# A streaming-encoder block: operands of the banded attention split for two heads at once and copied by DMA, values of the recurrence split in one piece

## The chip, the cores and the metric

The kernel runs on one core of one Trainium2 chip. The metric is the device time of one execution in microseconds. The core has a matmul engine (TensorE, "PE" in the profile, its weight load "PEld"), a vector engine (VectorE, "DVE"), a scalar engine (ScalarE, "ACT"), GpSimd ("POOL") and SyncE ("SP"), which only starts transfers. Each engine works through its own instructions in order; semaphores hold an instruction until what it needs is done. Sixteen DMA engines do the transfers. SBUF is the on-chip memory of 128 partitions, PSUM the accumulator memory that matmuls write.

## What is computed

One layer of a hybrid block, for 512 frames of width 1024. From the reference, cut to the two branches that the change touches:

```python
h = rmsnorm(x, norm_mix_g[l])
proj = h @ w_in[l]
...
y_a = chunked_relpos_attention(a_q, a_k, a_v, rel_bias[l])
y_b = hgrn2_recurrence(b_q, b_f, b_i, b_g, lb_all[l], hgrn_norm_g[l])
y_c = mla_attention(c_q, c_kv, c_kr, positions, ...)
up = jnp.einsum('bsnw,nwd->bsnd', branches, w_branch[l])
gates = jax.nn.sigmoid(gate_logits.reshape(bsz, seq, N_BRANCH, D_MODEL))
x = x + jnp.sum(gates * up, axis=2) @ w_out[l]
h2 = rmsnorm(x, norm_ffn_g[l])
x = x + jnp.square(jax.nn.relu(h2 @ w_ff1[l])) @ w_ff2[l]
```

The banded branch (A) has eight heads of width 64. Its scores, per chunk of 64 queries, carry a bias by relative position:

```python
s = jnp.einsum('bqhd,bkhd->bhqk', q_blk, k_band).astype(jnp.float32) * scale + bias
...
p = jax.nn.softmax(s, axis=-1).astype(v.dtype)
return jnp.einsum('bhqk,bkhd->bqhd', p, v_band)
```

The recurrence (B) has eight heads too and works on chunks:

```python
state = (jnp.exp(last[:, :, 0, :])[..., None] * state
         + jnp.einsum('bhjd,bhjv->bhdv', k_b * jnp.exp(last - cum), v_b))
```

## The kernel before

**Precision.** Every matmul runs on pairs: an operand is split into a rounded high half (ScalarE copies it to the matmul type) and a low half (VectorE subtracts the high half from the source). `split` (L209) does both; three matmuls, high by high, high by low and low by high, give a product.

**Order.** TensorE's order is written out by hand. The projections, gates and branch outputs are cut into units of one or two matmuls, and `fill(n)` puts the next n of them between the steps of a branch, so that TensorE has dense work while a branch waits for other engines. The other engines' orders are made by a scheduler from the program's order, its priorities and its model of times; a tile pool with `bufs=n` gives out n buffers in turn, and an instruction that writes a buffer waits for the last readers of its former content. Weights come through GpSimd's queue: `load` and `convert` bring a block twice, the second time added onto the negated high half, which leaves the low half.

**The stretches.** The latent branch (C) runs first, to about 166 us of the span; then the banded branch (A), to about 272 us; then the recurrence (B), to about 500 us; then the output projection and the feed-forward part. During C and A, `fill` works on projections, during B on gates and branch outputs.

**A branch's heads** go through `attention` (L566). A step is one head and one of four blocks of 128 queries, t = 0 to 3, with 128(t+1) keys. A step does the scores (`scores_step`, L516): matmuls into the PSUM tile `sc`, then VectorE adds the bias table and takes the row minimum (`sb`, L529), ScalarE takes the exponential and the row sum (`p`, L532); VectorE normalises later (L536, L537). Two steps behind, `transpose_step` (L540) transposes `p` through PSUM tiles `tp` and splits them into `pTh` (ScalarE) and `pTl` (VectorE). When all four blocks of a head are transposed, `value_step` (L554) multiplies by the values into a PSUM tile `av`, which ScalarE and VectorE add up into `ya` (L563, L564; `yc` in the latent branch). `tp` and `av` share two PSUM buffers.

**The operands of a banded head** are made by `prep_a` (L789). A projection gives queries and keys of a pair of heads in one tile of 128 partitions each (`aqk`), a head in each half. A head's query tile (`QT`, four of them, shared with the latent branch) holds the high half of the scaled queries in one half of the partitions and the low half in the other; its key tiles (`KT`, two for each parity of the head) hold the high half twice, and the low half twice. So one matmul of 128 partitions does two of the products. `prep_a(h + 2)` is called when the last block of head h has its scores issued, and is used a head later. It also brings the head's bias table (128 KB) by SyncE into one of two buffers, and VectorE negates it in place (L804), fills its left half (L805) and masks a corner (L806). The buffer is free when L529 of head h, t = 3, has read the old table.

**The values** of A and B come from `project_nat` (L445) as four tiles `nat`, one for each block of 128 frames, of 512 channels. A's are split into `v2` before the banded heads. B's are split in `ew_keys` (L1021), once for each pair of heads, block by block, into `vh` and `vl`.

Of the kernel before, what the change touches and what calls it, by code (L numbers as in the profile page):

```python
# [9 lines left out]
F32 = mybir.dt.float32  # L10
F32R = mybir.dt.float32r
I32 = mybir.dt.int32
AF = mybir.ActivationFunctionType
ALU = mybir.AluOpType
# [3 lines left out]
S = 512  # L18
P = 128
NK = D // P  # L20
NST = S // P
# [4 lines left out]
SC_A = 0.125  # L26
# [112 lines left out]
def _body(ctx, tc, ap, dbgo):  # L139
    nc = tc.nc  # L140
    V, A, G, T = nc.vector, nc.scalar, nc.gpsimd, nc.tensor
# [6 lines left out]
    def f(t):  # L148
        return t.bitcast(F32)
# [12 lines left out]
    def acc(n="acc"):  # L162
        return ps.tile([P, S], F32, tag="acc", name=n, bufs=3)
# [45 lines left out]
    def split(hi, lo, src):  # L209
        A.copy(hi, src)  # L210
        V.tensor_tensor(lo, src, f(hi), ALU.subtract)
# [121 lines left out]
    with ExitStack() as st_ctx:  # L333
# [10 lines left out]
        for k in range(NK):  # L344
            t = st.tile([P, S], F32, tag="xt", name="xt", bufs=8)
# [75 lines left out]
        for i in range(4):  # L421
            t = fqt(f"c{i}")
# [22 lines left out]
        def project_nat(src, name, pool, out, halves=(0, 1)):  # L445

            def half_run(half):
                def run():
                    pz = [acc("pv").rearrange("p (a c) -> p a c", a=2) for _ in range(2)]
                    for k in range(NK):  # L450
                        if k % 4 == 0:
                            wh, wl = get()
                        c = slice(k % 4 * 256, k % 4 * 256 + 256)
                        for s in range(NST):
                            q = slice(s * P, (s + 1) * P)
                            mm3(pz[s // 2][:, s % 2], xg[k][0][:, q], xg[k][1][:, q], wh[:, c], wl[:, c],
                                k == 0 and s % 2 == 0, k == NK - 1, skip_group_check=True)
                            if s < 3 or k < NK - 1:
                                yield from (1, 1)[s % 2:]
                    for s in range(NST):  # L460
                        if half == 0:
                            out.append(pool[0].tile([P, S], F32, tag="nat", name=name, bufs=4))
                        A.activation(out[s][:, half * 256:half * 256 + 256], pz[s // 2][:, s % 2], AF.Copy,
                                     scale=rstdn[:, s:s + 1])
                    yield 1
                return run
            for half in halves:
                last = add([src[half, kk] for kk in range(2)], half_run(half))
            return last
# [123 lines left out]
    with ExitStack() as at_ctx:  # L593
# [137 lines left out]
        with ExitStack() as a_ctx:  # L731
            app = a_ctx.enter_context(tc.tile_pool(name="apool", bufs=2, reuse_waits="tile"))
            v2 = []
            for s in range(NST):
                t = ab.tile([P, 8, P], F32R, tag="v2", name="v2a", bufs=4)
                split(t[:, :, 0:64], t[:, :, 64:128], avn[s].rearrange("p (h d) -> p h d", d=64))
                v2.append(t)
            nat_stack.close()
            lsp = ls_stack.enter_context(tc.tile_pool(name="lsp", bufs=1, side="right", reuse_waits="tile"))
# [46 lines left out]

            aops = {}

            def prep_a(h):  # L789
                pr, par = h // 2, h % 2  # L790
                q, k = aqk[2 * pr], aqk[2 * pr + 1]
                a = slice(par * 64, par * 64 + 64)
                o = slice(64 - par * 64, 128 - par * 64)
                q1 = QT[h % 4]
                k1, k2 = KT[2 * par], KT[2 * par + 1]
                A.activation(q1[a], q[a], AF.Copy, scale=-SC_A)
                V.scalar_tensor_tensor(q1[o], q[a], -SC_A, f(q1[a]), ALU.mult, ALU.subtract)
                A.copy(k1[a], k[a])
                A.copy(k1[o], k[a])
                V.tensor_tensor(k2[a], k[a], f(k1[a]), ALU.subtract)  # L800
                V.tensor_copy(k2[o], f(k2[a]))
                bias = app.tile([P, S], F32, tag="bias", name="bias", bufs=2)
                nc.sync.dma_start(bias[:, 256:], ap['rel'][h])
                V.tensor_scalar(bias[:, 256:], bias[:, 256:], -1.0, None, ALU.mult)  # L804
                V.tensor_scalar(bias[:, :256], relc[:, h:h + 1].to_broadcast([P, 256]), -1.0, None, ALU.mult)  # L805
                V.memset(bias[0:64, S - 64:S], -NEG)  # L806
                aops[h] = [(q1, k1), (q1, k2)], (bias, app)
# [11 lines left out]
    with ExitStack() as h_ctx:  # L819
# [103 lines left out]
        def items(pr):  # L923
# [97 lines left out]
            def ew_keys():  # L1021
                vh = st['vh'] = hp.tile([P, 4, P], F32R, name="vh", bufs=1)
                vl = st['vl'] = hp.tile([P, 4, P], F32R, name="vl", bufs=1)
                for c in range(4):
                    split(vh[:, c], vl[:, c], bvn[c][:, vs])
                d = st['dk'] = hw("dk", 384)
                G.tensor_tensor(d.rearrange("p (c i) -> p c i", i=P), cv[:, 0:3, P - 1:P].to_broadcast([P, 3, P]),
                                cv[:, 0:3], ALU.subtract)
                A.activation(d, d, AF.Exp)
                V.tensor_tensor(d, d, kk[:, :384], ALU.mult)  # L1030
                el = st['el'] = hp.tile([P, 4], F32, tag="el", name="el")
                A.activation(el, cv[:, :, P - 1], AF.Exp)
# [247 lines left out]
```

## Time and profile before

| what | value |
|---|---|
| median of three runs | 961.58 us (961.29 to 964.99) |
| the profiled execution | 962.54 us |
| its span, from first to last instruction | 960.8 us |
| mean granted TensorE clock | 0.991 |
| HBM traffic | 114.05 MB read, 2.16 MB written |

The forecast is worked out against the profiled execution, which took 1.74 us more than its span and 0.96 us more than the median. The page cuts the span into 40 slices of 24 us. A digit is the busy share of a slice in tenths (9 is 90% or more), `PEclk` the granted clock, DMA the mean busy share of the 16 DMA engines.

```profile
PE   8889999988998999999999999999999999999995
PEld 6578898977877788888778888888888888888995
DVE  6488888777878969788562554544322234446745
ACT  7557778777766667667552443443322234342311
POOL 4422101111144434342122013000000000000032
PEclk9999999999999999999999999999999999999998
DMA  6865445655666474758689623223223232322402
```

Slices 0 to 6 are the start and the latent branch, 7 to 11 the banded branch, 12 to 20 the recurrence, the rest the feed-forward part. TensorE is at 90% or more in most slices; VectorE is at 70 to 90% up to slice 18. The parts of the page that carry the prediction, and the answers of the trace behind them, stand there.

### The profile page before, as it was taken

How to read it: one execution, taken by the hardware profiler on the slowest of the kernel's cores; microseconds unless marked ns; L12 is line 12 of the kernel's file. 1: busy time of each engine (PE TensorE's matmuls, PEld its weight loads, DVE VectorE, ACT ScalarE, POOL GpSimd, SP SyncE). 2: the span in 40 equal slices, each digit the busy share in tenths (PEclk: the TensorE clock that was granted, in tenths of full speed). 3: DMA queues.
4: the chain of work that ended last, by engine and by line, in shares of the span. 5: the costliest groups of instructions: out<-in, count | busy, mean ns of one | idle time of the engine just before them, and what ended most of it. 6: DMA issues, size and time to landing. Idle time of an engine off the chain costs nothing.

```text
span 960.8 us, 12589 instructions
## 1 busy us (share of the span) xinstructions
PE 919.2 (96%) x4682; PEld 774.6 (81%) x4682; DVE 595.2 (62%) x1134; ACT 494.5 (51%) x911; POOL 183.2 (19%) x248
## 2 busy tenths in 40 slices
PE   8889999988998999999999999999999999999995
PEld 6578898977877788888778888888888888888995
DVE  6488888777878969788562554544322234446745
ACT  7557778777766667667552443443322234342311
POOL 4422101111144434342122013000000000000032
PEclk9999999999999999999999999999999999999998
DMA  6865445655666474758689623223223232322402
GB/s 198 212 136 124 89 82 114 138 116 121 139 131 134 102 165 104 161 125 193 136 209 203 158 87 101 97 88 110 88 97 100 88 110 88 100 97 88 154 1 88
DMA packets 37181, 117.04 MB, mean 122 GB/s; under 512 B 4416, under 2 KB 8656, under 8 KB 37120
## 3 DMA queue, kind: packets, MB, share of 16 engines
q0 software_dynamic: 18496, 67.17, 33.3%
q1 hardware_dynamic: 18624, 49.06, 15.8%
q8 instruction: 37, 0.61, 0.3%
q14 instruction: 24, 0.20, 0.1%
HBM read 114.05 MB, written 2.16 MB: 121 GB/s over the span
## 4 chain that ended last, share of the span: by engine, by line
PE 69%; DVE 14%; issue 7%; DMA 4%; ACT 3%; POOL 2%; SPq 0%; DVEq 0%; POOLq 0%; ACTq 0%
PE p L226 12%; PE p L224 12%; PE p L225 12%; PE pg L323 3%; PE pg L319 3%; PE pg L321 3%; PE pj L323 2%; PE pj L319 2%; PE pj L321 2%; DMA bias<-in_rel 2%; PE sc L520 2%; PE po L225 2%; PE po L226 2%; PE po L224 2%; PE tp L545 1%
## 5 line engine op out<-in xcount | busy, mean ns | idle before, releaser
L220 DVE TENSOR_TENSOR wl<-wr,wh 128x1024 fp32r<-128x1024 f32 x66 | 80.8, 1224 | 144.7 <-ACT wh L219 140.6
L219 ACT CAST wh<-wr 128x1024 fp32r<-128x1024 f32 x66 | 69.5, 1053 | 173.9 <-PE p L225 136.4
L224 PE MATMUL p<-x2h,wh 128*128 128x512 f32 x256 | 100.0, 391 | 0.0
L226 PE MATMUL p<-x2h,wl 128*128 128x512 f32 x256 | 99.6, 389 | 0.0
L225 PE MATMUL p<-x2l,wh 128*128 128x512 f32 x256 | 99.6, 389 | 0.0
L277 ACT ACTIVATE wl<-wh 128x1024 fp32r<-128x1024 f32 x64 | 67.8, 1059 | 49.7 <-PE pg L323 28.1
L224 PE MATMUL p<-rh,wh 128*128 128x512 f32 (+1 forms) x224 | 83.7, 374 | 0.0
L225 PE MATMUL p<-rl,wh 128*128 128x512 f32 (+1 forms) x224 | 83.7, 374 | 0.0
L226 PE MATMUL p<-rh,wl 128*128 128x512 f32 (+1 forms) x224 | 83.7, 374 | 0.0
L323 PE MATMUL pg<-xgh,wl 128*128 128x512 f32 x192 | 76.9, 401 | 0.6 <-DMA wl<-in_w_g 0.6
L1261 POOL TENSOR_TENSOR xres<-xres,cst 128x256 f32<-128x256 f32 x16 | 13.1, 822 | 335.7 <-ACT fss L1256 309.6
L319 PE MATMUL pg<-xgh,wh 128*128 128x512 f32 x192 | 76.7, 400 | 0.0
L321 PE MATMUL pg<-xgl,wh 128*128 128x512 f32 x192 | 76.4, 398 | 0.0
L319 PE MATMUL pj<-xgh,wh 128*128 128x512 f32 x160 | 64.6, 404 | 2.6 <-ACT c L427 2.6
L321 PE MATMUL pj<-xgl,wh 128*128 128x512 f32 x160 | 65.4, 408 | 0.0
L323 PE MATMUL pj<-xgh,wl 128*128 128x512 f32 x160 | 64.0, 400 | 1.3 <-DMA wl<-in_w_aqk 1.3
L225 PEld LDWEIGHTS p<-x2l,wh 128*128 128x128 f32 x256 | 48.1, 188 | 10.2 <-issue 0.2
L224 PEld LDWEIGHTS p<-x2h,wh 128*128 128x128 f32 x256 | 48.1, 188 | 10.1 <-issue 0.2
L226 PEld LDWEIGHTS p<-x2h,wl 128*128 128x128 f32 x256 | 48.1, 188 | 10.0
L225 PEld LDWEIGHTS p<-rl,wh 128*128 128x128 f32 x224 | 42.2, 188 | 7.5
L226 PEld LDWEIGHTS p<-rh,wl 128*128 128x128 f32 x224 | 42.2, 188 | 7.5
L224 PEld LDWEIGHTS p<-rh,wh 128*128 128x128 f32 x224 | 42.2, 188 | 7.4
(380 smaller groups left out, 2398.0 us busy)
## 6 DMA issues: line engine op xcount, KB each, us to landing
wr<-in_w_ff SPq DMA_DIRECT2D x64, 512.0 KB, 3.3
wh<-in_w_g POOLq DMA_DIRECT2D x24, 512.0 KB, 4.0
wl<-in_w_g POOLq DMA_DIRECT2D x24, 512.0 KB, 5.9
wh<-in_w_br POOLq DMA_DIRECT2D x12, 512.0 KB, 3.7
wl<-in_w_br POOLq DMA_DIRECT2D x12, 512.0 KB, 5.7
wh<-in_w_aqk POOLq DMA_DIRECT2D x8, 512.0 KB, 4.5
wl<-in_w_aqk POOLq DMA_DIRECT2D x8, 512.0 KB, 6.6
wr<-in_w_out SPq DMA_DIRECT2D x8, 512.0 KB, 3.3
```

The lines of the kernel that those rows point to most:

```text
L219: A.copy(hi[:, :n], r[:, :n])
L220: (eng or G).tensor_tensor(lo[:, :n], r[:, :n], f(hi[:, :n]), ALU.subtract)
L224: T.matmul(out, wh, xh, start=start, stop=False, **kw)
L225: T.matmul(out, wh, xl, start=False, stop=False, **kw)
L226: T.matmul(out, wl, xh, start=False, stop=stop, **kw)
L277: A.activation(lo, f(hi), AF.Copy, scale=-1.0)
L319: T.matmul(out, wh, xh, start=start, stop=False, **kw)
L321: T.matmul(out, wh, xl, start=False, stop=False, **kw)
L323: T.matmul(out, wl, xh, start=False, stop=stop, **kw)
L520: T.matmul(sc[:, :n], l[:, t * P:(t + 1) * P], r[:, :n], start=i == 0, stop=i == len(scores) - 1)
L545: T.transpose(tp[:, o * P:(o + 1) * P], p[:, kt * P:(kt + 1) * P], ident)
L1261: G.tensor_tensor(x2[m][:, n], x2[m][:, n], g_fin[:, m:m + 1].to_broadcast([P, 256]), ALU.mult)
```

## The change

**Banded branch.** A new `split_a` splits queries and keys of a pair of heads in tiles of 128 partitions: the scaled high half and the low half of the queries (`aqh`, `aql`), high and low half of the keys (`akh`, `akl`). The tiles come from a pool of eight buffers, two pairs' worth. `prep_a` no longer computes operands. Six SyncE transfers of 64x512 elements (128 KB) for each head copy them from the pair's tiles to where the head's matmuls read them: one for each half of the query tile, two for each key tile. The bias table is brought as before, behind these in the program.

**Values.** `project_nat` writes one tile with four blocks of frames instead of four tiles; the reader of A's values follows. `ew_keys` splits the values of a pair of heads in one go of 128x512 instead of four of 128x128.

```diff
             def half_run(half):
                 def run():
+                    if half == 0:
+                        out.append(pool[0].tile([P, NST, S], F32, tag="nat", name=name, bufs=1))
...
                     for s in range(NST):
-                        if half == 0:
-                            out.append(pool[0].tile([P, S], F32, tag="nat", name=name, bufs=4))
-                        A.activation(out[s][:, half * 256:half * 256 + 256], pz[s // 2][:, s % 2], AF.Copy,
+                        A.activation(out[0][:, s, half * 256:half * 256 + 256], pz[s // 2][:, s % 2], AF.Copy,
                                      scale=rstdn[:, s:s + 1])
...
-                split(t[:, :, 0:64], t[:, :, 64:128], avn[s].rearrange("p (h d) -> p h d", d=64))
+                split(t[:, :, 0:64], t[:, :, 64:128], avn[0][:, s].rearrange("p (h d) -> p h d", d=64))
...
+            def split_a(pr):
+
+                q, k = aqk[2 * pr], aqk[2 * pr + 1]
+                qh, ql, kh, kl = late['a'] = [app.tile([P, S], F32R, tag="as", name=n, bufs=8)
+                                              for n in ("aqh", "aql", "akh", "akl")]
+                A.activation(qh, q, AF.Copy, scale=-SC_A)
+                V.scalar_tensor_tensor(ql, q, -SC_A, f(qh), ALU.mult, ALU.subtract)
+                split(kh, kl, k)
+
             def prep_a(h):
+
                 pr, par = h // 2, h % 2
-                q, k = aqk[2 * pr], aqk[2 * pr + 1]
+                if par == 0:
+                    split_a(pr)
+                qh, ql, kh, kl = late['a']
                 a = slice(par * 64, par * 64 + 64)
                 o = slice(64 - par * 64, 128 - par * 64)
                 q1 = QT[h % 4]
                 k1, k2 = KT[2 * par], KT[2 * par + 1]
-                A.activation(q1[a], q[a], AF.Copy, scale=-SC_A)
-                V.scalar_tensor_tensor(q1[o], q[a], -SC_A, f(q1[a]), ALU.mult, ALU.subtract)
-                A.copy(k1[a], k[a])
-                A.copy(k1[o], k[a])
-                V.tensor_tensor(k2[a], k[a], f(k1[a]), ALU.subtract)
-                V.tensor_copy(k2[o], f(k2[a]))
+                nc.sync.dma_start(f(q1[a]), f(qh[a]))
+                nc.sync.dma_start(f(q1[o]), f(ql[a]))
+                for dst, src in ((k1, kh), (k2, kl)):
+                    nc.sync.dma_start(f(dst[a]), f(src[a]))
+                    nc.sync.dma_start(f(dst[o]), f(src[a]))
...
-                for c in range(4):
-                    split(vh[:, c], vl[:, c], bvn[c][:, vs])
+                split(vh, vl, bvn[0][:, :, vs])
```

The change lengthens the file: from `split_a` on, line numbers are higher (the negation of the bias is L804 before and L815 after, the scaled query copy L796 and L794, the transfers L808 to L812). Three engines' orders carry the argument.

**VectorE, the boundary behind the third banded head.** `sb` is the sum of scores and bias (its second row reads the minimum), `ls`, `bz` and `lm` belong to the forget gates of the recurrence, `ri` and `p` are the normalisation, `pTl` the low halves of a transposed tile. Before, from the last read of the old table on:

```order
L529 ISA sb_2397,mn_2395<-sc_2392,bias_2087 128x512
L529 ISA mn_2395 128x1
L800 TENSOR_TENSOR kt1_488<-aqk_951,kt0_487 64x512
L805 TENSOR_SCALAR bias_2436<-cst_71 128x256
L770 SCALAR_TENSOR_TENSOR ls_2347<-bz_2341,e_2343 128x512
L536 RECIPROCAL ri_2401<-sm_2399 128x1
L801 CAST kt1_488<-kt1_488 64x512
L771 SCALAR_TENSOR_TENSOR bz_2341<-bz_2341,e_2343 128x512
L537 TENSOR_SCALAR p_2396<-p_2396,ri_2401 128x512
L804 TENSOR_SCALAR bias_2436<-bias_2436 128x256
L564 TENSOR_TENSOR ya_1885<-av_2411,avl_2420 64x512
```

The negation L804 stands ahead of `ya`. The same place in the changed kernel, from the filling of the bias's left half on:

```order
L816 TENSOR_SCALAR bias_2454<-cst_71 128x256
L770 SCALAR_TENSOR_TENSOR ls_2357<-bz_2351,e_2353 128x512
L536 RECIPROCAL ri_2411<-sm_2409 128x1
L771 SCALAR_TENSOR_TENSOR bz_2351<-bz_2351,e_2353 128x512
L537 TENSOR_SCALAR p_2406<-p_2406,ri_2411 128x512
L776 TENSOR_SCALAR ls_2357<-ls_2357,lm_1886 128x512
L564 TENSOR_TENSOR ya_1882<-av_2421,avl_2430 64x512
L529 ISA sb_2473,mn_2471<-sc_2468,bias_2272 128x128
L529 ISA mn_2471 128x1
L211 TENSOR_TENSOR pTl_482<-tp_2433,pTh_481 128x2x128
L815 TENSOR_SCALAR bias_2454<-bias_2454 128x256
```

The two key instructions are gone, and the negation (now L815) has moved behind `ya`, the next head's first `sb` and a `pTl`. At the other five boundaries it stands behind `ya` (where there is one) and that `sb` too.

**SyncE, the same boundary and the next.** Before, the queue holds nothing but the bias tables there; the last five:

```order
L803 DMA bias_2087<-in_rel 128x256
L803 DMA bias_2262<-in_rel 128x256
L803 DMA bias_2436<-in_rel 128x256
L803 DMA bias_2607<-in_rel 128x256
L803 DMA bias_2767<-in_rel 128x256
```

In the changed kernel, from one bias table to the next:

```order
L814 DMA bias_2454<-in_rel 128x256
L808 DMA qt2_485<-aqh_2779 64x512
L809 DMA qt2_485<-aql_2780 64x512
L811 DMA kt2_489<-akh_2442 64x512
L812 DMA kt2_489<-akh_2442 64x512
L811 DMA kt3_490<-akl_2443 64x512
L812 DMA kt3_490<-akl_2443 64x512
L814 DMA bias_2625<-in_rel 128x256
```

Two query transfers need only free buffers; four key transfers wait for a head's last scores, and the bias table now follows them in the queue.

**ScalarE, the end of the latent branch.** `avl` and `pTh` are the copies of the last latent heads, `avn` the values of the banded branch on their way out of PSUM. Before:

```order
L532 ACTIVATE p_1774,sm_1777<-sc_1769,mn_1773 128x512
L563 COPY avl_1801<-av_1792 64x512
L210 CAST pTh_481<-tp_1804 128x2x128
L463 ACTIVATE avn_1573<-pv_1592,rstdn_83 128x256
L463 ACTIVATE avn_1575<-pv_1592,rstdn_83 128x256
L210 CAST pTh_481<-tp_1829 128x3x128
```

In the changed kernel:

```order
L532 ACTIVATE p_1771,sm_1774<-sc_1766,mn_1770 128x512
L563 COPY avl_1798<-av_1789 64x512
L210 CAST pTh_481<-tp_1801 128x2x128
L210 CAST akh_2442<-aqk_951 128x512
L463 ACTIVATE avn_1250<-pv_1589,rstdn_83 128x256 x2
L210 CAST pTh_481<-tp_1826 128x3x128
```

The keys of the third pair (`akh`) are split here, ahead of `avn` and of a `pTh` of the latent branch; the four single-head instructions of ScalarE that stood ahead of the first row (L796, L798, L799, L796) are gone.

## The prediction, made before the changed kernel ran

> **What bounds the kernel now.** The first view is the page's table of busy time. TensorE (PE) is busy for nearly the whole span, so a change is worth what it takes out of TensorE's idle time, or costs what it adds there, however much VectorE (DVE) or ScalarE (ACT) work it removes.
>
> ```profile
> PE 919.2 (96%) x4682; PEld 774.6 (81%) x4682; DVE 595.2 (62%) x1134; ACT 494.5 (51%) x911; POOL 183.2 (19%) x248
> PE 69%; DVE 14%; issue 7%; DMA 4%; ACT 3%; POOL 2%; SPq 0%; DVEq 0%; POOLq 0%; ACTq 0%
> ```
>
> The second line is the head of the chain that ended last: 4% of it, some 38 us, is waiting for a DMA. The next view cuts the time into the stretches that the edits touch: the end of the latent branch (140 to 166.5 us), seven of the eight banded heads (166.5 to 256), the banded tail, and the recurrence (272 to 500). Columns: stretch, its length, busy time of PE, PEld, DVE, ACT and POOL, granted clock, DMA share.
>
> ```profile
> 140.00:166.50 26.50, 24.29 (x182) 22.59 (x181) 22.22 (x71) 22.35 (x54) 4.24 (x6) 1.00 0.44 100
> 166.50:256.00 89.50, 82.21 (x511) 72.93 (x510) 71.23 (x214) 69.06 (x151) 13.69 (x19) 1.00 0.60 127
> 272.00:500.00 228.00, 220.31 (x1118) 184.08 (x1117) 178.36 (x315) 148.77 (x296) 84.88 (x126) 0.99 0.67 144
> ```
>
> PE idles 89.50 - 82.21 = 7.3 us in the banded heads, 2.2 before them, 7.7 in the recurrence. These 17 us are all that the change can win; nothing outside them reads what it edits. What ended the idle time, for the banded heads (PE, then DVE):
>
> ```profile
> PE tp L545 <- DVE ya L564: 5.4, 3, 2.6
> PE tp L545 <- DVE p L537: 0.7, 1, 0.7
> PE tp L545 <- DVE pTl L211: 0.6, 1, 0.6
> PE tp L545 <- DVE ri L536: 0.6, 1, 0.6
> DVE bias L804 <- DMA bias<-in_rel: 8.1, 4, 3.0
> ```
>
> All four PE rows have DVE behind them, and DVE's own longest wait is for the bias table. The timeline at one head boundary shows the link (start, duration; idle time and its releaser in brackets):
>
> ```profile
> 200.76 0.08 DVE L529 DVE_READ_ACCUMULATOR2_ANT mn<- 128x1 f32 x1
> 200.81 0.68 DVE L800 TENSOR_TENSOR kt<-aqk,kt 64x512 fp32r<-64x512 f32 x1
> ...
> 206.73 0.29 DVE L804 TENSOR_SCALAR bias<-bias 128x256 f32<-128x256 f32 x1 [2.78 <-DMA bias<-in_rel]
> 207.05 0.69 DVE L564 TENSOR_TENSOR ya<-av,avl 64x512 f32<-64x512 f32 x1
> ```
> ```profile
> 199.47 0.63 PE L520 MATMUL sc<-kt,qt 128*128 128x512 f32 x2
> 200.87 0.33 SPq L803 DMA_DIRECT2D bias<-in_rel  x1
> 207.79 0.55 PE L545 MATMUL tp<-ident,p 128*128 128x128 f32 x3 [2.08 <-DVE ya L564]
> DMA to landing us min/median/max: 2.0/4.1/5.8
> ```
>
> The bias transfer can start only when the old table has been read (200.84) and lands 5.8 us later. DVE works in order, so `ya`, which needs no bias, stands behind L804; the transposes need the PSUM buffer that `ya` frees. So **a late DMA stops DVE, and DVE stops PE**. The eight bias transfers took 2.0 to 5.8 us.
>
> **The banded edit: what goes and what comes.**
>
> ```profile
> L796 ACT ACTIVATE qt<-aqk x8: 628/632/647, 146.7 to 220.4; 64x512 fp32r<-64x512 f32 x8
> L797 DVE SCALAR_TENSOR_TENSOR qt<-aqk,qt x8: 685/686/689, 148.1 to 221.1; 64x512 fp32r<-64x512 f32 x8
> L798 ACT CAST kt<-aqk x8: 605/616/632, 147.2 to 242.1; 64x512 fp32r<-64x512 f32 x8
> L800 DVE TENSOR_TENSOR kt<-aqk,kt x8: 677/686/690, 148.9 to 243.2; 64x512 fp32r<-64x512 f32 x8
> L801 DVE CAST kt<-kt x8: 421/422/423, 151.6 to 244.3; 64x512 fp32r<-64x512 f32 x8
> 300.00 0.62 ACT L210 CAST kxh<-d 128x512 fp32r<-128x512 f32 x1 [1.38 <-DVE d L995]
> 301.86 0.69 DVE L211 TENSOR_TENSOR kxl<-d,kxh 128x512 fp32r<-128x512 f32 x1
> ```
>
> L799 repeats L798. Gone: on DVE 8 x (0.69 + 0.69 + 0.42) = 14.4 us, on ACT 8 x (0.63 + 0.62 + 0.62) = 15.0. The last two rows say that 128 partitions cost the same as 64, so a pair's split costs 2 x 0.69 on DVE and 2 x 0.62 on ACT: 5.5 and 5.0 come back. The order puts seven of the eight splits of each engine into the end of the latent branch, where the first four heads' operands were made anyway (DVE 7 x 0.69 = 4.8 us for 5.0 before). The banded heads themselves lose nearly all: DVE about 9 of 71.2 us, ACT about 9 of 69.1. Against PE's 82.2 that is slack, not time; by itself it wins nothing.
>
> Added: 48 SyncE transfers of 128 KB (6.3 MB). Operands for head h+2 leave when head h's last scores are done and are needed one head later, about 12 us (89.5 us for a good seven heads); the slowest SyncE row above is 5.8, so they are hidden by a whole head of work.
>
> **The wait that goes, and what is late next.** The order in the section on the change shows that `ya` now stands ahead of the negation of the bias, as do the next head's first sums and the low halves of two transposed tiles. So the 5.4 us of `ya` go. What stands behind the negation now is the next tile's normalisation and the low halves that free the buffer for a later transpose:
>
> ```profile
> 212.80 0.27 PE L545 MATMUL tp<-ident,p 128*128 128x128 f32 x1
> ```
>
> Without its 2.08 and 0.55 us of idle time PE would reach this transpose at 210.2. DVE needs about 1.4 us after the landing (0.29 negation, then normalisation and low halves), so the bias must land by 208.8, 7.9 us after 200.87. It now queues behind four operand transfers: they are released by the scores at 200.1, and at 0.33 us of issue each the bias leaves at 201.4, 0.55 later; that is the lower end (landing 207.3, no stall). For the upper end the four must move first, 512 KB:
>
> ```profile
> wr<-in_w_ff SPq DMA_DIRECT2D x64, 512.0 KB, 3.3
> ```
>
> which gives 207.3 + 3.3 = 210.6, 1.8 us too late. The chain names the three slowest landings at the four boundaries where DVE waits now (start, duration):
>
> ```profile
> 176.59 4.47 DMA bias<-in_rel
> ...
> 200.87 5.83 DMA bias<-in_rel
> ...
> 227.59 5.52 DMA bias<-in_rel
> ```
>
> With 0.55 + 3.3 more, 5.83 is 1.8 over the 7.9, 5.52 is 1.5 over, 4.47 is 0.4 over, and faster ones are under. So PE keeps 0 to 3.7 us of idle time; I take 1.8, the middle, which also has to cover `ya` now standing behind L776. **Banded heads: -7.3 + 1.8 = -5.5 us, ends -7.3 and -3.6.**
>
> The Trainium skill, page "DMA: Bandwidth & Descriptors", section "Anatomy of one DMA", puts a transfer at about 2.0 us plus its bytes over 436 GB/s; for 640 KB on one queue that is an estimate of 3.5 us, and the term would be its full -7.3. The trace disagrees for one single bias transfer: median 4.1 us where the formula gives 2.3. The fastest of the eight (2.0 us) agrees.
>
> **The end of the latent branch.** The pair's four tiles come from eight buffers, so pair 2's keys (`akh`, `akl`) must wait until pair 0's have been copied, the last to head 1's operands, which are released by the last latent scores:
>
> ```profile
> 155.68 0.86 PE L520 MATMUL sc<-kt,qt 96*128 96x512 f32 x3
> 162.04 0.55 PE L545 MATMUL tp<-ident,p 128*128 128x128 f32 x3 [0.47 <-DVE yc L564]
> 161.25 0.84 ACT L463 ACTIVATE avn<-pv,rstdn 128x256 f32<-128x256 f32 x2 [0.54 <-PE pv L226]
> 162.62 0.48 ACT L210 CAST pTh<-tp 128x384 fp32r<-128x384 f32 x1 [0.53 <-PE tp L545]
> 164.38 0.50 PE L561 MATMUL av<-pTh,v 128*128 128x512 f32 x1 [0.99 <-ACT pTh L210]
> ```
>
> Scores end at 156.5, the fourth transfer is issued by 157.5 and lands at 159.5 (2.0 us) to 163.3 (5.8). ACT holds `akh`, then two exports of the value projection (`avn`, 0.84 us), then `pTh` in this order: 0.62 + 0.84 after the landing is 161.0 to 164.8 for a `pTh` that starts at 162.62 now. Queued behind it are the last transposes' halves and PE's last latent values. The `yc` wait of 0.47 goes, since 2.5 us of ACT work at that place go. Ends -0.5 and +2.2; at the median landing (161.6, `pTh` at 163.1) **+0.5 us**, the value taken.
>
> **The recurrence edit.** Per pair, four splits of 128x128 become one of 128x512:
>
> ```profile
> L210 ACT CAST vh<-bvn x16: 292/294/299, 275.9 to 430.9; 128x128 fp32r<-128x128 f32 x16
> L211 DVE TENSOR_TENSOR vl<-bvn,vh x16: 272/284/3909, 279.9 to 432.2; 128x128 fp32r<-128x128 f32 x16
> PE sl L224 <- ACT d L986: 2.7, 1, 2.7
> 287.80 3.83 DVE vl L211
> ```
>
> DVE saves 4 x (4 x 0.284 - 0.69) = 1.8 us, ACT 4 x (4 x 0.294 - 0.62) = 2.2, out of 178 and 149 busy in a stretch where PE waits 7.7 us for one of them. Most of it lies beside PE's dense work. On the path lies the 2.7 us wait in the first pair, which ends a chain of DVE work that holds three of these instructions, the last of them in the last row (its median is 0.28, so most of the 3.83 us is standing still and may fall on the next instruction instead); 3 x 0.28 = **0.8 us** is taken off it. Ends: -2.7 (the whole wait) and +0.8, if the slightly moved order costs what it was to win. The one tile for four sequence blocks computes the same in the same places: nothing.
>
> **Weight transfers.** 6.3 MB beside a DMA share of 0.60: PE waits for no weight in the banded stretch, and for one by 1.3 us at most elsewhere; I take 0, ends 0 and +1.3.
>
> ```profile
> PE pj L323 <- DMA wl<-in_w_aqk: 1.3, 1, 1.3
> ```
>
> **Sum.** -5.5 + 0.5 - 0.8 + 0 = -5.8 us. Against the profiled execution (962.54 us, 1.74 of it around the span of 960.8) that is 956.7. The median of the runs, 961.58, is 0.96 lower; the forecast for the median is **955.8 us**.
>
> **The rivals.**
> - *The wait only moves* (0.23): the negation lands late at every boundary and PE stands at the later transpose instead of at `ya`. For: DVE still stops in order, and the transfer starts later. Against: the 7.9 us of room. With 1.2 us lost at each of six boundaries, -7.3 + 7.2 + 0.5 - 0.8 = -0.4: 961.2 us.
> - *Slower* (0.10): the operand transfers fill SyncE's queue so that the bias lands 10 us after the old table is read. Each of six boundaries then costs 10 - 7.9 = 2.1 us, 12.6 in all, and the latent tail its 2.2: -7.3 + 12.6 + 2.2 - 0.8 = +6.7, 968.3 us. It decides from about 7.9 + 7.3 / 6 = 9.1 us of landing on. Against it: the slowest SyncE row for 128 KB is 5.8.
> - *All of it goes* (0.12): no stall at the negation, none in the latent tail, and the recurrence wait gone: -7.3 - 0.5 - 2.7 = -10.5, 951.1 us. For: DVE's load in the heads falls to about 62 of 82 us. The formula of the Trainium skill's page "DMA: Bandwidth & Descriptors" ("Anatomy of one DMA") would give the first of these three terms.
>
> **How the numbers follow.** The forecast case (955.8, from 953 to 959) has 0.55. A change of 0.5% (4.8 us) is about what a measurement of this kernel can tell from none; below 956.8 lie some two thirds of the forecast case and the third rival: faster 0.48. Same: the rest and the first rival, 0.42. Slower 0.10. The range leaves out the slow rival and the far end of the fast one: 951 to 963.
>
> **What would show it.** Right: no PE row `tp <- ya` in the banded heads; DVE still with some microseconds at the bias; bias transfers of 5 to 8 us; PE idle about 2 us in the heads; DVE about 9 us less busy there. Wrong: PE rows of transposes behind `pTl` or `p` of 5 us and more (the first rival); ACT waiting for `kt` transfers by more than 2 us near 160 us; DMA rows of `kt` and `qt` above 8 us; PE waiting for weights.

## The result, and the profile after

| | runs | median | range |
|---|---|---|---|
| before | 11 | 962.70 us | 960.89 to 966.99 |
| after | 11 | 971.74 us | 964.42 to 976.07 |

The ratio is 1.008, with a 95% interval of 1.0059 to 1.0102: the changed kernel is slower by 0.8%, and the forecast of 955.8 us (951 to 963) was wrong. Here and below a ratio compares undisturbed runs only, so it can differ a little from the quotient of two medians. The changed kernel also spreads over 12 us where the kernel before spreads over 6. The execution that was profiled is its fastest, 964.42 us (span 962.6); two more traces, of 966.63 and 977.97 us, are read further down.

The page of that fastest run: the engines' busy time.

```profile
PE 919.4 (96%) x4682; PEld 774.8 (80%) x4682; DVE 584.1 (61%) x1106; ACT 483.4 (50%) x883; POOL 185.4 (19%) x248
```

VectorE and ScalarE each lost 11 us of work, as the diff says, and the span did not follow. The first two stretches again (length, busy time of PE, PEld, DVE, ACT, POOL, granted clock, DMA share), and what ended the idle time in the banded heads:

```profile
140.00:166.50 26.50, 22.63 (x174) 21.42 (x172) 19.81 (x67) 19.02 (x50) 3.37 (x5) 0.98 0.75 167
166.50:256.00 89.50, 84.88 (x507) 74.44 (x508) 62.90 (x196) 61.23 (x137) 14.55 (x20) 0.97 0.80 172
```
```profile
PE tp L545 <- DVE p L537: 2.7, 2, 2.3
PE av L561 <- ACT pTh L210: 2.4, 1, 2.4
PE tp L545 <- DVE pTl L211: 1.0, 2, 0.6
PE tp L545 <- DVE ya L564: 0.8, 2, 0.6
DVE bias L815 <- DMA bias<-in_rel: 7.8, 4, 3.0
```

The wait for `ya` fell from 5.4 to 0.8 us, as forecast. VectorE still stands 7.8 us at the bias, and PE now waits behind `p`, `pTl` and `pTh` instead. In the second stretch the clock is 0.97 where it was 1.00, and the DMA engines are busy for 0.80 of it, where it was 0.60.

**The end of the latent branch.** Timeline of ScalarE and PE there, the DMA wait that the chain names, and two windows of 4 us (PE's idle time and its releaser in brackets):

```profile
157.41 0.63 ACT L794 ACTIVATE aqh<-aqk 128x512 fp32r<-128x512 f32 x1 [2.56 <-issue]
163.68 0.62 ACT L210 CAST akh<-aqk 128x512 fp32r<-128x512 f32 x1 [1.09 <-DMA kt<-akh]
...
164.93 0.48 ACT L210 CAST pTh<-tp 128x384 fp32r<-128x384 f32 x1
162.96 0.55 PE L545 MATMUL tp<-ident,p 128*128 128x128 f32 x3 [1.23 <-DVE yc L564]
166.68 0.79 PE L561 MATMUL av<-pTh,v 128*128 128x512 f32 x1 [2.38 <-ACT pTh L210]
156.87 6.10 DMA kt<-akh
```
```profile
164.00:168.00 4.00, 1.62 (x6) 0.85 (x5) 1.85 (x3) 4.00 (x9) 0.66 (x2) 0.70 0.72 193
168.00:172.00 4.00, 4.00 (x13) 3.47 (x12) 3.69 (x6) 2.96 (x6) 0.75 (x1) 0.50 0.67 102
```

The third pair's split (`aqh`, then `akh`) waits for buffers that transfers still read. At `akh` the trace names the transfer: ScalarE goes on at 163.68, behind a key transfer that took 6.10 us from 156.87. At `aqh` it stands 2.56 us and the trace names no releaser; that a query transfer still read this buffer is inferred. ScalarE is in order, so `pTh` follows at 164.93 and PE stands 2.38 us, shortly after a wait of 1.23. What the forecast did not contain is the second window: PE is busy all of it, at **half its clock**. It issues 13 matmuls there, where the kernel before issued 22 in the same window:

```profile
168.00:172.00 4.00, 4.00 (x22) 3.40 (x21) 2.74 (x9) 1.02 (x4) 0.00 (x0) 1.00 0.57 108
```

The matmuls of the two windows are not all the same, but projection matmuls of one kind (L319, L321, L323) follow each other every 0.43 us there and every 0.23 us before. The first `sb` of the banded branch starts at 173.3 us instead of 169.6.

**A head boundary.** VectorE and PE behind the bias transfer that was issued at 232.14 us:

```profile
238.22 0.29 DVE L815 TENSOR_SCALAR bias<-bias 128x256 f32<-128x256 f32 x1 [1.77 <-DMA bias<-in_rel]
...
239.23 0.67 DVE L436 TENSOR_TENSOR bq<-pj,rstd 128x512 f32<-128x512 f32 x1
239.82 1.36 DVE L783 TENSOR_TENSOR_SCAN cum<-ones,ls 128x128 f32<-128x128 f32 x4
...
241.54 0.28 DVE L537 TENSOR_SCALAR p<-p,ri 128x128 f32<-128x128 f32 x1
241.97 0.30 PE L545 MATMUL tp<-ident,p 128*128 128x128 f32 x1 [2.29 <-DVE p L537]
```

The old table's last read ended at 231.05 and the new one was negated at 238.22, 7.2 us later and inside the 7.9 us that the forecast allowed. PE stood 2.29 us all the same: from the start of the negation to that of the normalisation `p` VectorE had 3.3 us of work (most of it `ls`, `bq`, `cum` and `pTl`), where the forecast had counted 1.4 for all that PE needs.

### The profile page after: what moved, and what is told of

Same layout as the page of the kernel before. It is cut to its first block, busy times and chain, and to the rows that moved or that the text cites. A ratio compares the mean times of both kernels' runs of the same rounds, so it can differ in the third digit from the quotient of the medians.

```text
span 962.6 us, 12645 instructions
## 1 busy us (share of the span) xinstructions
PE 919.4 (96%) x4682; PEld 774.8 (80%) x4682; DVE 584.1 (61%) x1106; ACT 483.4 (50%) x883; POOL 185.4 (19%) x248
## 4 chain that ended last, share of the span: by engine, by line
PE 66%; DVE 13%; issue 8%; DMA 5%; ACT 4%; POOL 2%; SPq 1%; DVEq 0%; POOLq 0%; ACTq 0%
PE p L224 12%; PE p L225 12%; PE p L226 12%; PE pg L323 2%; PE pg L319 2%; PE pg L321 2%; PE pj L323 2%; PE pj L319 2%; PE pj L321 2%; PE sc L520 2%; DVE qbl L211 2%; PE po L225 2%; PE po L226 2%; PE po L224 2%; DMA bias<-in_rel 1%
## 5 line engine op out<-in xcount | busy, mean ns | idle before, releaser
L323 PE MATMUL pg<-xgh,wl 128*128 128x512 f32 x192 | 75.5, 393 | 0.9 <-DMA wl<-in_w_g 0.9
L319 PE MATMUL pg<-xgh,wh 128*128 128x512 f32 x192 | 75.5, 393 | 0.3 <-DVE tg L893 0.2
L321 PE MATMUL pg<-xgl,wh 128*128 128x512 f32 x192 | 75.3, 392 | 0.0
L319 PE MATMUL pj<-xgh,wh 128*128 128x512 f32 x160 | 65.9, 412 | 3.0 <-ACT c L427 3.0
L321 PE MATMUL pj<-xgl,wh 128*128 128x512 f32 x160 | 66.1, 413 | 0.0
L323 PE MATMUL pj<-xgh,wl 128*128 128x512 f32 x160 | 64.7, 404 | 1.4 <-DMA wl<-in_w_aqk 1.4
```

The lines of the kernel that those rows point to most:

```text
L319: T.matmul(out, wh, xh, start=start, stop=False, **kw)
L321: T.matmul(out, wh, xl, start=False, stop=False, **kw)
L323: T.matmul(out, wl, xh, start=False, stop=stop, **kw)
```

## The experiments

**1 and 2: which edit.** The first kernel is the changed one with the values of the recurrence as before; the second is the kernel before with the values edit alone.

> The changed kernel with the values as before (four tiles, four splits of 128x128): only the banded edit is left. If the loss comes from the banded edit (theories stall and traffic): 968 to 973 us, 6 to 10 above the kernel before. If it comes from the recurrence edit: 961 to 964.

Measured: 971.31 us (6 runs), ratio 1.0075 (1.0046 to 1.0104), with the same waits in the trace (`pTh` 2.0 us, `p` 2.6).

> The kernel before with only the values edit (one tile, one split of 128x512). Theories stall and traffic: 961 to 963 us, at most 1 below the kernel before. If the loss came from this edit: 968 and more.

Measured: 963.89 us (12 runs), ratio 1.0001 (0.9986 to 1.0016). The loss is the banded edit's. The values edit does nothing that can be measured.

**3: no buffer is reused.** The changed kernel, with the low halves written over their own source, so that the eight buffers hold all high halves and no split waits for a transfer:

```diff
-qh, ql, kh, kl = late['a'] = [app.tile([P, S], F32R, tag="as", name=n, bufs=8)
-                              for n in ("aqh", "aql", "akh", "akl")]
+qh, kh = [app.tile([P, S], F32R, tag="as", name=n, bufs=8) for n in ("aqh", "akh")]
+ql, kl = q.bitcast(F32R), k.bitcast(F32R)
+late['a'] = qh, ql, kh, kl
```

> The changed kernel, but the low halves overwrite the projections they are taken from, so that the eight buffers hold the high halves of all four pairs and no split waits until transfers have read a buffer. The same 48 transfers remain. Theory stall (ScalarE and VectorE stand at reused buffers near the end of the latent branch, TensorE idles 3.6 us there and its granted clock falls to half for some 6 us): 956 to 962 us, TensorE idle below 2 us between 156 and 168 us, granted clock 1.00 there, and the runs lie closer together than 964 to 976. Theory traffic (6.3 MB more make every transfer late): 968 to 973 us as the changed kernel, with the clock falling all the same.

Measured: 967.08 us (12 runs), ratio 1.0017 (0.9993 to 1.004). Its windows (the latent tail, then the one behind a head boundary) and its waits in the banded heads:

```profile
140.00:166.50 26.50, 24.31 (x183) 22.60 (x181) 22.24 (x72) 21.32 (x55) 3.37 (x5) 1.00 0.74 159
192.00:196.00 4.00, 4.00 (x20) 3.63 (x20) 3.13 (x11) 3.39 (x9) 0.54 (x1) 0.69 0.20 46
```
```profile
PE tp L545 <- DVE pTl L211: 5.8, 2, 4.3
DVE bias L816 <- DMA bias<-in_rel: 16.3, 5, 6.7
```

The latent tail is as dense as before (24.31 of 26.50 us, clock 1.00). What remains is VectorE standing 16.3 us at the bias, twice what it was, and a PE wait of 4.3 us with a low clock behind it. The time is neither theory's: above the 956 to 962 us of the stall, below the 968 to 973 us of the traffic, and within 0.4% of the kernel before.

**4: a third bias buffer.** The kernel before, with `bufs=3` for the bias tables.

> The kernel before with three buffers for the bias table instead of two, so that a head's table can be fetched a head earlier; no other change. If the wait of VectorE for the bias is what TensorE's 5.4 us of idle time in the banded heads come from, that idle time goes: 955 to 959 us, no wait of VectorE for bias transfers in the heads. If the wait only covers something else that is late as well: 960 to 963 us.

Measured: 961.82 us (12 runs), ratio 0.9981 (0.9965 to 0.9998). The waits in the heads, and VectorE at one boundary:

```profile
PE tp L545 <- DVE ya L564: 5.1, 3, 3.1
DVE bias L804 <- DMA bias<-in_rel: 6.5, 3, 3.5
234.59 0.29 DVE L804 TENSOR_SCALAR bias<-bias 128x256 f32<-128x256 f32 x1 [3.45 <-DMA bias<-in_rel]
235.51 0.68 DVE L564 TENSOR_TENSOR ya<-av,avl 64x512 f32<-64x512 f32 x1
```

The idea failed: the last transfer now starts a head earlier, at 228.60, but the scheduler put its negation forward with it, and `ya` stands behind it as before. The gain is some 0.2%, in the range of the second expectation.

**5 and 6: the bias off VectorE.** The three instructions on the table go to GpSimd, in the kernel before (5) and in the kernel of experiment 3 (6); the third `memset` line likewise:

```diff
-V.tensor_scalar(bias[:, 256:], bias[:, 256:], -1.0, None, ALU.mult)
-V.tensor_scalar(bias[:, :256], relc[:, h:h + 1].to_broadcast([P, 256]), -1.0, None, ALU.mult)
+G.tensor_scalar(bias[:, 256:], bias[:, 256:], -1.0, None, ALU.mult)
+G.tensor_scalar(bias[:, :256], relc[:, h:h + 1].to_broadcast([P, 256]), -1.0, None, ALU.mult)
```

> The kernel before, with the three instructions on the bias table (negation, constant half, mask) moved from VectorE to GpSimd, so that VectorE no longer stands in front of the table's transfer. Theory (what the banded heads of before lose is VectorE standing at the bias): the wait of TensorE for ya (5.4 us) falls under 1 us, its idle time in the windows of the heads from 7.3 to 2 or 3 us, the time to 956 to 959 us. Rival (the wait only moves, to the first score row that reads the table, or to the weights queued on GpSimd): VectorE's idle time is then named at sb with GpSimd as releaser, 961 to 963 us.

Measured: **955.87 us** (6 runs), ratio 0.9914 (0.9893 to 0.9935), at the lower edge of the theory's 956 to 959. PE's wait for `ya` in the heads falls from 5.4 to 0.7 us.

> The changed kernel with the low halves made in place (as in the run that measured 967.08 us) and the three bias instructions on GpSimd. Theory (what was left of the loss, 5 us against the kernel before, is the late bias table in front of VectorE, and the clock that falls after the stalls): the 16.3 us of VectorE's waits for the bias are gone, PE's idle time in the heads falls to 3 us or less, no window of the heads has a granted clock under 0.95, 955 to 960 us. Rival (the 48 transfers cost by their load, wherever the bias is negated: score rows wait for the table or for operands): 964 us or more, with the waits named at sb or at the score matmuls.

Measured: **954.98 us** (6 runs), ratio 0.9919 (0.9895 to 0.9943). The banded heads of experiment 5, then those of 6 with GpSimd's wait there:

```profile
172.00:256.00 84.00, 83.31 (x526) 75.07 (x525) 71.20 (x204) 70.98 (x155) 30.76 (x40) 1.00 0.64 136
```
```profile
172.00:256.00 84.00, 84.00 (x529) 75.61 (x529) 63.35 (x192) 62.88 (x142) 29.47 (x40) 1.00 0.82 188
POOL bias L816 <- DMA bias<-in_rel: 35.4, 5, 9.0
```

In 6 the DMA engines are busy for 0.82 of the stretch and GpSimd waits 35.4 us for bias tables, and PE has no idle time at all. So neither the load of 48 transfers nor a late table costs anything that shows here; an engine that PE depends on, standing in order behind the table, does. And the two times agree: the 8 us that VectorE and ScalarE save in the heads bring nothing that shows.

**7: the transfers alone.** The kernel before, with 48 transfers of the same size out of the finished operands into tiles that nothing reads:

```diff
+for src in (q1, k1, k2):
+    spare = app.tile([P, S], F32, tag="as", name="spare", bufs=8)
+    nc.sync.dma_start(spare[a], f(src[a]))
+    nc.sync.dma_start(spare[o], f(src[o]))
 bias = app.tile([P, S], F32, tag="bias", name="bias", bufs=2)
```

> The kernel before, with 48 transfers of 64x512 out of the finished operands into a spare tile that nothing reads, ahead of the bias on SyncE's queue; no operand comes by a transfer. If the transfers cost by delaying the bias (queue and load): VectorE's waits for the bias rise from 8.1 us to 15 or more, 966 to 969 us, as in the run with the low halves in place. If the loss comes from operands that arrive late by transfer: within 0.3% of before, 961 to 964 us.

Measured: 966.60 us (12 runs), ratio 1.0029 (1.0014 to 1.0044). VectorE and PE in the heads:

```profile
DVE bias L808 <- DMA bias<-in_rel: 11.8, 6, 3.0
PE tp L545 <- DVE pTl L211: 3.7, 4, 1.3
```

This is between the two expectations: the time is in the range of the first, the ratio just inside the 0.3% of the second, and the wait for the bias rises from 8.1 to 11.8 us instead of 15 or more. Traffic delays the table, at a price of some 3 us, but less than in experiment 3. The queue is not the one of the changed kernel, though: at three of six boundaries (bias issued at 176.94, 204.02 and 230.93 us) the bias left SyncE ahead of two or three of the four transfers of key tiles that stand in front of it at the other three, so the experiment does not price the place in the queue.

**8: the bias on GpSimd's queue.** Experiment 3 with `nc.gpsimd.dma_start` for the table; VectorE still negates.

> The changed kernel with the low halves made in place and the bias fetched by GpSimd's queue instead of SyncE's; negation still on VectorE. If the bias is late because it stands behind four key transfers in SyncE's queue: it leaves within 1 us of its release and lands in 3 to 4 us, the waits for it fall from 16.3 to 8 us or less, 959 to 963 us. If it is late by the load of the DMA engines: landings stay at 5 to 7 us and the time at 965 to 968 us.

Measured: 967.27 us (12 runs), ratio 1.0042 (1.0022 to 1.0062). The eight transfers, and VectorE's wait in the heads:

```profile
DMA to landing us min/median/max: 2.8/4.6/6.8
DVE bias L816 <- DMA bias<-in_rel: 15.8, 6, 4.1
```

The table now leaves 0.3 us after the old one is read, and VectorE's longest wait falls from 6.7 to 4.1 us, but the sum stays (15.8 us against 16.3) and so does the time. Landings of 2.8 to 6.8 us are enough for that price, so the place behind four key transfers is not all of it; it goes with the longest waits. The experiment does not tell the two apart, because VectorE's order changed with it: at two boundaries (206.81 and 220.24 us) the negation stands ahead of `ya` again, and PE's longest wait, 4.0 us, is for `ya`.

**9: GpSimd in the changed kernel.** The edit of 5, in the changed kernel as it is.

> The changed kernel as it is (eight buffers for all four halves, so the splits of pair 2 wait for the transfers of pair 0), with the three bias instructions on GpSimd. Theory (two separate losses, the wait at the reused buffers in the latent tail and the late bias in front of VectorE; the first stays here): PE idle in the heads from 172 us on under 1 us, but 3 to 4 us of idle and a granted clock of 0.5 to 0.8 stay in 160 to 176 us; 957 to 962 us, 3 to 6 us above the run with the low halves in place and GpSimd. Rival (the wait at the buffers costs nothing of its own): 953 to 956 us, as that run. Rival (most of the loss of the changed kernel lies there): 964 us or more.

Measured: 962.35 us (12 runs), ratio 0.9996 (0.9978 to 1.0014). That is 0.35 us above the theory's range and some 7 us above experiment 6, where 3 to 6 were expected. The trace shows what stays: 3.7 us of idle PE from 160 to 172 us with the clock at 0.81 and then 0.50 from 164, and 1.4 us of idle PE from 176 to 256. This completes a table of ratios to the kernel before:

| banded operands | bias on VectorE | bias on GpSimd |
|---|---|---|
| per head (before) | 1 | 0.9914 |
| per pair, low halves in place | 1.0017 | 0.9919 |
| per pair, eight buffers for all (after) | 1.0080 | 0.9996 |

Each ratio has an interval of about 0.2 points to each side. Down a column, the reuse of the buffers costs 0.6 to 0.8% (6 to 7 us); the split per pair itself costs 0.2% or nothing. Across, the bias on VectorE costs 0.8 to 1.0% in every row, in the kernel before too. So the change did not remove the price of the late table, and what it lost against the kernel before is about what the reuse costs.

**10 and 12: more traces of the changed kernel.**

> The changed kernel once more, for the trace of an ordinary run (the profiled run of the result, 964.42 us, was the fastest of eleven; their median is 971.74). If the runs differ by the granted clock alone, an ordinary run shows the same waits at the same places, PE idle within 2 us of the fast one, and more windows under 0.9 granted clock, in the latent tail and the heads. If they differ by the transfers, the waits for the bias or for akh are longer by 5 us or more.

Measured: 966.63 us. The waits are at the same places. PE idles 2.5 us more than in the fastest trace, more windows have a low clock (four of 4 us under 0.9, where it was two), and VectorE waits 11.4 us for the bias, 3.6 more. Neither branch of the expectation fits whole: the runs differ by the clock and by the transfers, the transfers by less than 5 us.

> The changed kernel a third time, for the trace of a run near its median (971.7 us; the two traces so far are of 964.42 and 966.63 us). If the runs differ by when the bias lands and by the clock after it: the time above 966.6 us appears as PE idle and as windows under 0.9 granted clock between 176 and 256 us, and the rest of the program agrees within 1 us of PE busy. If by something else (a clock below 1.00 all through, later stages): between 176 and 256 us it stays within 1 us of the trace of 966.63.

Measured: 977.97 us (span 976.2). Its first boundary: SyncE's queue (issue time in the second column), the wait in the chain, VectorE and PE; then two windows.

```profile
181.34 0.82 SPq L812 DMA_DIRECT2D kt<-akh  x1
182.28 1.68 SPq L811 DMA_DIRECT2D kt<-akl  x1
184.40 0.46 SPq L812 DMA_DIRECT2D kt<-akl  x1
184.97 0.51 SPq L814 DMA_DIRECT2D bias<-in_rel  x1
184.97 7.04 DMA bias<-in_rel
181.03 0.69 DVE L529 CUSTOM_DVE_ANT_0 sb<-sc,bias 128x512 f32<-128x512 f32 x1 [0.29 <-PE sc L520]
192.04 0.29 DVE L815 TENSOR_SCALAR bias<-bias 128x256 f32<-128x256 f32 x1 [6.46 <-DMA bias<-in_rel]
193.59 0.48 PE L545 MATMUL tp<-ident,p 128*128 128x128 f32 x1 [4.02 <-DVE pTl L211]
207.62 0.69 DVE L211 TENSOR_TENSOR akl<-aqk,akh 128x512 fp32r<-128x512 f32 x1 [5.35 <-DMA kt<-akl]
209.43 0.33 PE L545 MATMUL tp<-ident,p 128*128 128x128 f32 x1 [2.48 <-DVE pTl L211]
```
```profile
192.00:196.00 4.00, 2.41 (x12) 2.41 (x12) 3.89 (x12) 0.75 (x3) 0.00 (x0) 0.69 0.30 59
252.00:256.00 4.00, 4.00 (x13) 3.19 (x13) 2.36 (x9) 1.41 (x4) 0.00 (x0) 0.63 0.30 67
```

The old table's read ended at 181.7, the bias left at 185.0 and was there at 192.0, 10.3 us later; PE stood 4.02 us. At the second boundary the fourth pair's `akl` waits 5.35 us for its buffer, ahead of the negation in VectorE's order, so the reuse strikes twice, and PE stands 2.48 us. Behind the first stall the clock falls to 0.69, behind the second to 0.82 and 0.75 (208 to 216 us). Of the 11.4 us between this span and that of the 966.63 us run, 7.6 had appeared by the last `sb` of the heads (277.9 against 270.3). The other 3.8 came later, so the second half of that expectation did not hold. They are in the recurrence: the clock fell there twice (0.62 from 312 us, 0.64 from 404, 3.4 us by the count of the table below), where the other trace has no such fall, and PE idled 0.8 us more. The kernel before has falls in its recurrence too (0.80 from 304 us, 0.69 from 368), so these are not shown to come from the change.

**11: more fill in the latent tail.** `TUNE` with `cd=9` instead of 6.

> The changed kernel with 9 instead of 6 units of projection work put into each step of the latent tail, so that TensorE has work while VectorE and ScalarE wait there. If the stall there and the fall of the granted clock after it are what this place costs: PE idle in 160 to 172 us falls from 3.6 to under 1.5 us, the clock stays at 1.00, and the time falls to 964 to 968 us. If the later heads lack the work that is used up here: no gain or a loss, 970 us or more, with PE idle in 240 to 276 us.

Measured: 973.66 us (11 runs), ratio 1.0097 (1.0065 to 1.0128). The first expectation missed: PE idled 3.6 us from 160 to 172 us as without the extra work, it was busy for 1.37 us of 164 to 168 us (1.62 without), the clock behind it was 0.50 again, and the time is no better. So this run does not show what a dense tail would be worth; experiment 3 does.

**All traces in one table.** First and last `sb` of the banded branch; PE idle, summed over 36 windows of 4 us from 140 to 284 us; and clock loss, the sum over the same windows of 4 us times (1 - granted clock). This counts too much where PE also stands, by up to 1.6 us in the trace of experiment 12.

| kernel | first, last `sb` | PE idle | clock loss | span |
|---|---|---|---|---|
| before | 169.6, 265.7 | 10.8 | 0.0 | 960.8 |
| after | 173.3, 267.7 | 9.8 | 3.4 | 962.6 |
| after (10) | 172.4, 270.3 | 12.3 | 5.2 | 964.8 |
| after (12) | 173.8, 277.9 | 15.7 | 8.6 | 976.2 |
| lows in place (3) | 171.3, 273.1 | 13.5 | 3.4 | 967.0 |
| before, GpSimd (5) | 171.0, 259.4 | 4.1 | 0.0 | 955.8 |
| lows in place, GpSimd (6) | 169.7, 257.3 | 3.1 | 0.0 | 952.2 |
| after, GpSimd (9) | 174.4, 264.8 | 7.0 | 3.4 | 960.5 |

Idle time and clock loss together account for the spans to within some 3 us: against before, the two sums differ by +2.4, +6.7, +13.5, +6.1, -6.7, -7.7 and -0.4 us, the spans by +1.8, +4.0, +15.4, +6.2, -5.0, -8.6 and -0.3.

## Why the prediction was wrong

- **What bounds the kernel** was right, and stronger than it was put: a late bias table stops VectorE, and VectorE stops PE. With the table off VectorE the kernel before is 0.9% faster, some 8 us (experiment 5); the forecast had counted 7.3 us as the heads' whole idle time.
- **"Slack, not time; by itself it wins nothing"** was right. VectorE fell from 71.2 to 62.9 us in the heads, ScalarE from 69.1 to 61.2, and experiments 5 and 6 end within 0.9 us of each other.
- **"So the 5.4 us of `ya` go"** was right, but they went elsewhere. The term of **-5.5 us for the banded heads is the one that failed**. From first to last `sb` the heads took 96.1 us before; after, 94.4, 97.9 and 104.1 us in the three traces, so -1.7, +1.8 and +8.0. That is not only the reuse of the buffers: experiment 3, without it, does not gain either (ratio 1.0017). Two steps of the term fell. "DVE needs about 1.4 us after the landing" left out the work that queues behind the negation while VectorE stands: 3.3 us at 238.22, and PE stood 2.29 us although the bias was in time. And the place in the queue: its lower end, 0.55 us of delay, used SyncE's issue time in a queue that held nothing but bias tables, 0.33 us. In the slowest trace's first boundary the four key transfers took 0.46 to 1.68 us each to issue, so the table left 3.3 us after the read; with its 7.04 us to landing that is 10.3. Over the six boundaries the table left 0.3 to 3.0 us after the read in the fastest trace, where it was 0.04 us before. The estimate of the full -7.3 was further off still: the Trainium skill's page "DMA: Bandwidth & Descriptors" gives that formula, in the section "Anatomy of one DMA", for transfers that GpSimd issues, and these leave by SyncE.
- **The operand transfers, "hidden by a whole head of work"** since "the slowest SyncE row above is 5.8", came in time for their own heads: no row of PE waits for one in the three traces of the changed kernel. But they were priced at nothing, and two things were left out: the buffers that they read and the queue that they fill. The 5.8 us row stands in a stretch with a DMA share of 0.60. A key transfer took 6.10 us where the share was 1.02 and 1.05 (156 to 164 us of the fastest trace), and a bias table 7.04 where it was 0.97 (184 to 192 us of the slowest), and the splits of the third and fourth pair waited for buffers that such transfers were reading. The bias tables alone did not land later in the fastest trace (2.2 to 6.1 us, median 4.0, against 2.0 to 5.8 and 4.1).
- **The latent tail, "+0.5 us", ends -0.5 and +2.2**: the mechanism was the right one (`akh` behind a key transfer, `pTh` behind `akh`), the size was not. The first `sb` moved by +3.7, +2.8 and +4.2 us. The `yc` wait of 0.47, which was to go, rose to 1.23. PE's added idle time up to 172 us is 1.8 us in the fastest trace; most of the rest is the clock, 0.70 and then 0.50. The fourth pair's wait for its buffers was not in the working at all. Both together are the 6 to 7 us by which experiments 3 and 6 beat their neighbours with eight buffers for all, nearly the whole 0.8%.
- **The recurrence, "-0.8 us"**: 1.0001, with an interval of about 1.5 us to each side; an 0.8 us gain can be neither seen nor excluded. **Weights, 0**: no row of PE in the heads waits for one; in the slowest trace one waits 2.4 us in the recurrence, above the end of 1.3.
- **The rivals.** "Slower", given 0.10, has the nearest number, 968.3 us, but only part of its mechanism is what happened. It wanted the bias 10 us after the old table's read at six boundaries. From that read to the negation it was 3.6 to 7.2 us in the fastest trace, 3.7 to 8.4 in that of 966.63 and 4.3 to 10.3 in the slowest, where two of the six came near 10 and one of these (9.9) stood behind `akl` and not behind the table; before, it was 2.1 to 5.9. Without the reuse of the buffers the change gives about the 961.2 us of "The wait only moves" (ratio 1.0017 in experiment 3); the 0.6 to 0.8% on top is the reuse, for which no rival had more than the tail's 2.2 us.
- **A term that was missing**: every price was taken as idle time alone. With a granted clock that falls after a stall, the slowest trace has 13.5 us more than the kernel before up to 284 us: 4.9 us of idle time and, counted as in the table, 8.6 us of clock.

## What to carry to other kernels

A transfer that replaces engine work must be priced at the DMA share and in the queue that it creates, not at those in the old trace, and every buffer that it reads stays taken until it lands; count the buffers for all that is in flight. Ask of each instruction that waits for a DMA which engine it stands on: on an engine that TensorE depends on, whatever is queued behind it waits too, while on an idle one (GpSimd here, 0.9% of the time for three moved lines) even 35 us of waiting were free. A third buffer did not help here, because the scheduler moved the consumer forward with the transfer.

## What the runs showed of the hardware

- **A short stall can lower the clock.** 2.38 us of waiting, 1.23 us shortly before it, were followed by a window at 0.50; a wait of 4.02 us by 0.69, waits of 2.48 and 2.69 us by 0.82 and 0.63. The length of one wait does not decide it: at the same boundary, the kernel before waited 2.64 us for `ya` (from 232 us) and kept its clock at 1.00, and in experiment 2 a wait of 2.48 us for `ya` came with 0.77 and then 0.81. What decides it is open. The Trainium skill, page "TensorE: Matmul & The Clock Gate", section "HAM oscillation — how this bites in real kernels", says that the clock falls for idle gaps over about 3.4 us. The trace fits it for the 4.02 us; for the others it does not, since the clock fell with no single gap that long.
- **Issue time on SyncE.** In the heads of the slowest trace a 64x512 transfer inside SBUF took 0.46 to 1.97 us to issue (to 2.64 us in the fastest), and a bias table behind them 0.51 to 0.68, where it took 0.33 to 0.42 in the kernel before.
- **Spread as a symptom.** The changed kernel's times spread over 12 us, and those of experiment 3 over 17; with the bias off VectorE the same two kernels spread over 8 and 6 us (experiments 9 and 6). That fits a table whose landing decides whether PE stalls, and a stall that costs clock besides; it was read from three traces, not shown run by run.
